# Two-layer decoder trunk: the second product of each SwiGLU by seven products of quarters

## The chip, the cores and the metric

The kernel runs on one core of one Trainium2 chip. The metric is the device time of one execution in microseconds. TensorE (PE) multiplies, VectorE (DVE) and ScalarE (ACT) do the work by elements, GpSimd (POOL) a little of the norms, and the queue of SyncE (SP) issues nearly all transfers.

## The reference, cut to what matters

The input is 512 tokens of width 1024; 16 learned meta tokens are put ahead of them, which makes 528. Two layers follow, each with a SwiGLU, a mixer and a second SwiGLU, and a last norm; the meta tokens are dropped at the end. All of it is float32.

```python
def swiglu(x, w_in, w_out):
    gate, up = jnp.split(x @ w_in, 2, axis=-1)
    return (jax.nn.silu(gate) * up) @ w_out          # D_FF = 2816

for i in range(DEPTH):                               # DEPTH = 2
    h = h + 0.5 * swiglu(rmsnorm(h, norm_ffn1[i]), ffn1_w_in[i], ffn1_w_out[i])
    hn = rmsnorm(h, norm_mix[i])
    mix = retention(hn, ...) if i == 0 else gla(hn, ...)
    h = h + mix
    h = h + 0.5 * swiglu(rmsnorm(h, norm_ffn2[i]), ffn2_w_in[i], ffn2_w_out[i])
h = rmsnorm(h, final_norm)
```

## The kernel before

The activations lie with their features on the 128 partitions and the tokens along the free axis: the residual stream `xa` is 8 row tiles of 128 x 528. The hidden layer of a SwiGLU has 22 such row tiles. The 528 tokens are taken as two halves of 264; the last SwiGLU, which needs no meta tokens, has halves of 256. The program has six stages, one after the other: the SwiGLU f10, the retention, the SwiGLUs f20 and f11, the gated linear attention, and the SwiGLU f21. The names of tiles carry these.

Every float32 product is made of three matmuls (`mm3`, L296 to L298): both factors are split into a high part and the rest, and high by high, high by rest and rest by high are added up in PSUM. The activations' parts are `uha` and `ula` (`hh` and `hl` of the hidden layer). The weights stream in by SP's queue as chunks of 128 x 1024 into four buffers (`raw`), and are split on the chip in pieces of 512 columns: ACT copies the high part (`whi`, L119) and DVE subtracts it (`wlo`, L120). Seven buffers of each part let this run up to seven pieces ahead of PE. One piece feeds four row tiles of the sum, which is 12 matmuls on one half of the tokens.

The first product of a SwiGLU (the gates `g` and the ups `u`) is taken as it stands for the first four hidden tiles. The other 18 tiles go in nine pairs by `unit`: two tiles by two halves of the tokens are a product of 2 x 2 quarters, and seven products of quarters and of their sums (Winograd's form) take the place of eight. The sums of weight quarters (`ws`, four for each unit, L105) are made by DVE ahead of the split, and those of the activations (`t_sums`) once for each SwiGLU. The three banks X, Y and Z take the products, and DVE and ACT put the quarters of the result together as they come. A pair of tiles, gate and up, is 2 x 7 pieces, or 168 matmuls.

The second product (`out_steps`) is taken as it stands: the 22 hidden tiles are cut into `GROUPS` of four or two, and for each group and each of the 8 row tiles of the result there is a step of 24 matmuls (12 for the group of two) into `po_f`, after which DVE adds half of it to `xa` (L670). The steps of a group lie between the quarters of the next group's units (`mid`, and after the unit), and those of the last group at the end, where each row tile of `xa` becomes final and `feed` makes the next stage's `uha` and `ula` (L367, L369) and the squares of the norm (L377) from it. The order on each engine is that of the program, except that what stands in `urgent()` is moved ahead of other ready work by the tile scheduler.

## Time and profile before

| | before |
|---|---|
| median of 3 runs | 2157.18 us (2157.05 to 2157.83) |
| profiled execution, its own time | 2157.2 us |
| its span | 2155.8 us |
| PE busy | 2138.7 us, 99% |
| DVE busy | 1699.6 us, 79% |
| ACT busy | 990.6 us, 46% |
| POOL busy | 20.8 us, 1% |

The profiled execution's time is that of the median run, and its span is 1.4 us shorter than it. Busy time is the time in which at least one instruction of the engine runs. The page's 40 slices show PE at nine tenths or more in all but the first and the last, and the granted clock of PE at nine tenths or more in all of them.

### The profile page before, as it was taken

What the parts mean: (1) busy time and instruction counts of PE and PEld (TensorE: products, weight loads), DVE (VectorE), ACT (ScalarE), POOL (GpSimd) and SP (SyncE); (2) the same over time, 40 slices, a digit from 0 to 9 for tenths busy, and PEclk for the clock granted to TensorE, in tenths of its full rate; (3) what the DMA queues carried; (4) which work ended last, traced back from release to release, by engine and by line L of the source; (5) the groups of instructions that cost most, each with busy time, mean ns of one, the idle gap of its engine ahead of it and who ended that gap; (6) DMA issues with size and microseconds to landing.
All of it is one profiled execution on the core that took longest, in us unless ns stands there. A gap on an engine that the chain in (4) does not pass through costs nothing.

```text
span 2155.8 us, 42829 instructions
## 1 busy us (share of the span) xinstructions
PE 2138.7 (99%) x17454; PEld 2121.4 (98%) x17454; DVE 1699.6 (79%) x3105; ACT 990.6 (46%) x1843; POOL 20.8 (1%) x25
## 2 busy tenths in 40 slices
PE   8999999999999999999999999999999999999998
PEld 8999999999999999999999999999999999999998
DVE  7887787977676788798787878787775659798886
ACT  5454445444444454454444444444633234454444
POOL 0000000000000000000000000000000000000000
PEclk9999999999999999999999999999999999999999
DMA  4333334232323222333333233333321122333332
GB/s 147 99 107 95 104 99 131 71 99 79 99 79 99 79 79 60 98 104 103 99 94 113 70 96 102 108 99 100 107 70 59 60 77 71 94 103 99 108 99 79
DMA packets 71844, 201.28 MB, mean 93 GB/s; under 512 B 8032, under 2 KB 13536, under 8 KB 71648
## 3 DMA queue, kind: packets, MB, share of 16 engines
q1 hardware_dynamic: 70640, 195.26, 29.8%
q10 hardware_dynamic: 1008, 3.29, 0.5%
q8 instruction: 137, 2.24, 0.4%
q14 instruction: 59, 0.48, 0.1%
HBM read 196.42 MB, written 2.10 MB: 92 GB/s over the span
## 4 chain that ended last, share of the span: by engine, by line
PE 97%; DVE 2%; ACT 1%; issue 0%; POOL 0%; DMA 0%; POOLq 0%; DVEq 0%; ACTq 0%
PE po_f L296 8%; PE po_f L297 8%; PE po_f L298 8%; PE po_r L298 1%; PE po_r L296 1%; PE po_r L297 1%; PE lv L1147 1%; PE po L296 1%; PE gv L296 1%; PE pk L296 1%; PE pk L297 1%; PE gv L298 1%; PE gv L297 1%; PE pk L298 1%; PE gg L296 1%; PE gg L298 1%
## 5 line engine op out<-in xcount | busy, mean ns | idle before, releaser
L119 ACT CAST whi<-raw 128x512 fp32r<-128x512 f32 (+1 forms) x653 | 397.2, 610 | 595.7 <-PE gv L297 50.0
L120 DVE TENSOR_TENSOR wlo<-raw,whi 128x512 fp32r<-128x512 f32 (+1 forms) x653 | 437.7, 673 | 94.4 <-ACT whi L119 89.5
L297 PE MATMUL po_f<-hlf,whi 128*128 128x264 f32 (+1 forms) x1344 | 380.8, 283 | 0.0
L296 PE MATMUL po_f<-hhf,whi 128*128 128x264 f32 (+1 forms) x1344 | 380.8, 283 | 0.0
L298 PE MATMUL po_f<-hhf,wlo 128*128 128x264 f32 (+1 forms) x1344 | 380.3, 283 | 0.0
L119 ACT CAST whi<-ws 128x512 fp32r<-128x512 f32 x344 | 213.1, 621 | 341.3 <-PE po_f L297 91.7
L120 DVE TENSOR_TENSOR wlo<-ws,whi 128x512 fp32r<-128x512 f32 x344 | 235.4, 685 | 23.5 <-ACT whi L119 21.4
L298 PEld LDWEIGHTS po_f<-hhf,wlo 128*128 128x128 f32 x1344 | 253.0, 188 | 0.0
L296 PEld LDWEIGHTS po_f<-hhf,whi 128*128 128x128 f32 x1344 | 253.0, 188 | 0.0
L297 PEld LDWEIGHTS po_f<-hlf,whi 128*128 128x128 f32 x1344 | 252.7, 188 | 0.0
L670 DVE SCALAR_TENSOR_TENSOR xa<-po_f,xa 128x528 f32<-128x528 f32 (+1 forms) x184 | 129.1, 701 | 109.4 <-PE po_f L298 108.7
L105 DVE TENSOR_TENSOR ws<-raw 128x512 f32<-128x512 f32 x86 | 59.3, 689 | 36.3 <-DMA raw<-in_f_in 36.2
L298 PE MATMUL po_r<-ogh,wlo 128*128 128x264 f32 x256 | 73.0, 285 | 0.0
L296 PE MATMUL po_r<-ogh,whi 128*128 128x264 f32 x256 | 72.9, 285 | 0.0
L297 PE MATMUL po_r<-ogl,whi 128*128 128x264 f32 x256 | 72.6, 284 | 0.0
L324 ACT CAST hhf<-uf 128x528 fp32r<-128x528 f32 (+1 forms) x88 | 55.3, 628 | 31.8 <-DVE uf L624 21.4
L325 DVE TENSOR_TENSOR hlf<-uf,hhf 128x528 fp32r<-128x528 f32 (+1 forms) x88 | 61.4, 699 | 3.9 <-ACT hhf L324 1.4
L105 DVE TENSOR_TENSOR ws<-ws,raw 128x512 f32<-128x512 f32 x86 | 59.0, 686 | 0.8
L105 DVE TENSOR_TENSOR ws<-raw,ws 128x512 f32<-128x512 f32 x86 | 58.8, 683 | 0.4
L105 DVE TENSOR_TENSOR ws<-raw,raw 128x512 f32<-128x512 f32 x86 | 58.7, 683 | 0.1
L296 PEld LDWEIGHTS po_r<-ogh,whi 128*128 128x128 f32 x256 | 48.3, 189 | 0.0
L297 PEld LDWEIGHTS po_r<-ogl,whi 128*128 128x128 f32 x256 | 48.3, 189 | 0.0
(647 smaller groups left out, 7065.0 us busy)
## 6 DMA issues: line engine op xcount, KB each, us to landing
raw<-in_f_in SPq DMA_DIRECT2D x176, 512.0 KB, 3.5
raw<-in_f_out SPq DMA_DIRECT2D x160, 256.0 KB, 2.7
raw<-in_ret_in SPq DMA_DIRECT2D x48, 512.0 KB, 3.5
raw<-in_gla_in SPq DMA_DIRECT2D x25, 512.0 KB, 3.5
raw<-in_ret_o SPq DMA_DIRECT2D x16, 512.0 KB, 3.5
raw<-in_f_out SPq DMA_DIRECT2D x32, 128.0 KB, 2.2
raw<-in_gla_o SPq DMA_DIRECT2D x8, 512.0 KB, 3.4
xa<-in_xT SPq DMA_DIRECT2D x8, 264.0 KB, 5.1
```

The source lines that it names most:

```text
L105: op(t, a, b)
L119: self.nc.scalar.copy(hi[:, :n], raw[:, :n])
L120: self.nc.vector.tensor_sub(lo[:, :n], raw[:, :n], hi[:, :n].bitcast(F32))
L296: nc.tensor.matmul(ps, lhsT=lh, rhs=rh, start=start, stop=False, **kw)
L297: nc.tensor.matmul(ps, lhsT=lh, rhs=rl, start=False, stop=False, **kw)
L298: nc.tensor.matmul(ps, lhsT=ll, rhs=rh, start=False, stop=stop, **kw)
L324: S.copy(hi, src)
L325: V.tensor_sub(lo, src, hi.bitcast(F32))
L670: ins = V.scalar_tensor_tensor(xv, ps[d][:, :, :wd], scale, xv, ALU.mult, ALU.add)
L1147: nc.tensor.matmul(ps[:, j, J * P:J * P + n], lhsT=Kt[:, j, J * P:(J + 1) * P], rhs=q, start=(J == 0), stop=(J == 3), skip_group_check=True)
```

## The change

The second product is taken by units of seven as well. The hidden tiles are cut into groups of 8, 8 and 6 (`GROUPS`; the last SwiGLU has 6, 6, 6 and 4, and its last group stays as it was, in `out_last`). The first four tiles of a SwiGLU are still computed as they stand (`NPL`). For a group, four units (`unit_o`) make the 8 row tiles of the result in pairs, each of 7 pieces with as many row tiles of the sum as the group has pairs of tiles: 4, 4 and 3, so a piece is 12 or 9 matmuls and 512 or 384 columns of weights. `ffn_steps` writes the order out: the four units of a group stand in a row between the gate unit and the up unit of the next group's first pair, and those of the last group at the end.

For this the hidden layer is needed as quarters: for each pair of tiles `hidden` now makes four sums of quarters on DVE (`t_sums`) and splits seven quarters in place of two tiles. The form of the seven is another one, for all units, those of the retention too: of weight quarters only sums are taken, X is one bank in which `a11`, `s2`, `s3` and `a22` are added up one after the other, and Q and Z are a pair of banks. ACT copies X after `a11` and after `s2`, and Z after `s1`; DVE reads X after `s3` (`c22`), the pair of banks after `s4` (`row1`), and X again after `a22` (`c21`). The matmuls of `a22` go into X and so follow the reading by `c22`; between `s3` and `a22` lies the piece `s4`.

In the retention, the steps of the scores (`steps`) stand ahead of the gates for every head; so far they stood inside the first gate unit for head 0. The rows of `w_out` lie in DRAM in the new order, with fewer and larger transfers: SP issues 395 where it issued 483.

```diff
-GROUPS = ((0, 4), (4, 6), (6, 10), (10, 14), (14, 18), (18, 22))
+GROUPS = ((0, 8), (8, 16), (16, 22))
+LAST_GROUPS = ((0, 6), (6, 12), (12, 18), (18, 22))
+NPL = 4
...
-    UNIT = ("a11", "s2", "s1", "s3", "a12", "s4", "a22")
-    FIRST = ("s2", "s1", "a11", "s3", "a12", "s4", "a22")
+    UNIT = ("a11", "s1", "s2", "a12", "s3", "s4", "a22")
+    FIRST = ("s1", "s2", "a11", "a12", "s3", "s4", "a22")
+    SUMS = {"s1": ("a21", "a22"), "s2": ("s1", "a11"), "s3": ("a11", "a21"), "s4": ("a12", "s2")}
...
+    def ffn_steps(last):
...
+        for gi, (f0, f1) in enumerate(groups):
+            for f in range(max(f0, NPL), f1, 2):
+                steps.append(("i", "g", f))
+                steps += outs
+                outs = []
+                steps.append(("i", "u", f))
+            plain = last and gi == len(groups) - 1
+            outs = [("l" if plain else "o", gi, d) for d in range(0, KD, 1 if plain else 2)]
+        return steps + outs
...
+                if kind == "o":
+                    W.add_unit(key, w_out[layer, b_, :, c], w_out[layer, b_ + 1, :, c], W.UNIT)
...
+    WITH = {"a11": ("n11", "X"), "s1": ("t1", "Z"), "s2": ("t2", "X"), "a12": ("n21", "Q"), "s3": ("n3", "X"),
+            "s4": ("n22", "Z"), "a22": ("t4", "X")}
...
+        for q in W.FIRST if first else W.UNIT:
+            what, into = WITH[q]
             w = W.get(key + (q,))
...
+                if q == "s1":
+                    S.copy(su[:, 2], to["Z"])
+                elif q == "a11":
+                    S.copy(su[:, int(first)], X)
+                    if first:
+                        V.tensor_sub(su[:, 0], su[:, 1], su[:, 3])
+                elif q == "s2":
+                    S.copy(su[:, 3 if first else 1], X)
+                elif q == "s3":
+                    c22(X, su[:, 2])
+                elif q == "s4":
+                    row1(su[:, :2], QZ)
+                elif q == "a22":
+                    c21(X)
...
-        for q in (W.FIRST if first else W.UNIT)[:3]:
-            quarter(q, *{"a11": ("X", "b11"), "s2": ("Y", "t2"), "s1": ("Z", "t1")}[q])
...
-        mid()
-        quarter("s3", "Y", "t3")
-        with urgent():
-            V.tensor_add(u3, ps["Y"], s1)
-        quarter("a12", "X", "b21")
-        with urgent():
-            done(0, 0, None, ps["X"])
-        quarter("s4", "Z", "b22")
-        with urgent():
-            done(0, 1, ps["Z"], u2)
-            done(1, 1, u3, s5)
-        quarter("a22", "Y", "t4")
-        with urgent():
-            done(1, 0, ps["Y"], s1)
...
+                    split(hi[:, 4], lo[:, 4], y[:, 0, a0:a1])
+                    t_sums(up_, f"{me}h{f}", halves, y[:, 0], y[:, 1], h[:, 0, :4], h[:, 1, :4])
+                    split(hi[:, 5:], lo[:, 5:], pair(y[:, 1], halves))
...
+            def unit_u(f, g):
...
+                def row1(ab, qz):
+                    o = pair(y[0][:, 0], halves)
+                    V.tensor_add(o, ab, qz)
+                    V.tensor_mul(o, o, pair(g[0], halves))
...
+                def c22(c, s):
+                    y.append(gated(f))
+                    o = y[0][:, 1, b0:b1]
+                    V.tensor_add(o, c, s)
+                    V.scalar_tensor_tensor(o, o, -1.0, g[1][:, b0:b1], ALU.mult, ALU.mult)
...
+                def c21(c):
+                    V.scalar_tensor_tensor(y[0][:, 1, a0:a1], c, -1.0, g[1][:, a0:a1], ALU.mult, ALU.mult)
...
+            def unit_o(gi, d):
...
+                def row1(ab, qz):
+                    o = pair(x[d], halves)
+                    V.scalar_tensor_tensor(o, ab, -0.5, o, ALU.mult, ALU.add)
+                    ins = V.scalar_tensor_tensor(o, qz, -0.5, o, ALU.mult, ALU.add)
+                    if feed and gi == len(groups) - 1:
+                        feed(d, ins)
...
+                def c22(c, s):
+                    o = x[d + 1][:, b0:b1]
+                    V.scalar_tensor_tensor(o, s, 0.5, o, ALU.mult, ALU.add)
+                    V.scalar_tensor_tensor(o, c, 0.5, o, ALU.mult, ALU.add)
...
+                def c21(c):
+                    o = x[d + 1][:, a0:a1]
+                    ins = V.scalar_tensor_tensor(o, c, 0.5, o, ALU.mult, ALU.add)
+                    if feed and gi == len(groups) - 1:
+                        feed(d + 1, ins)
```

Two places show how the instructions move. The first is DVE's queue in the middle of the SwiGLU f20, at the end of an up unit: `Xf20u`, `Yf20u`, `Zf20u` and `QZf20u` are PSUM, `suf20u` is the copies of quarters in SBUF, `uf` and `yf` are gated hidden tiles, and `gf` the gates. Before:

```order
L120 TENSOR_TENSOR wlo_12993<-ws_208_12990,whi_12992 128x512
L624 TENSOR_TENSOR uf_12761<-uf_12761,gf_12556 128x264
L623 TENSOR_TENSOR uf_12762<-Yf20u_12764,suf20u_12766 128x264
L120 TENSOR_TENSOR wlo_13010<-raw_12746,whi_13009 128x512
L624 TENSOR_TENSOR uf_12762<-uf_12762,gf_12557 128x264
L325 TENSOR_TENSOR hlf_12967<-uf_12761,hhf_12966 128x528
L325 TENSOR_TENSOR hlf_12967<-uf_12762,hhf_12966 128x528
L670 SCALAR_TENSOR_TENSOR xa<-po_f_12934,xa 128x528
L120 TENSOR_TENSOR wlo_13029<-ws_208_13026,whi_13028 128x512
```

After:

```order
L640 TENSOR_TENSOR yf_12833<-suf20u_12739,QZf20u_12738 128x528
L122 TENSOR_TENSOR wlo_12924<-ws_168_12921,whi_12923 128x512
L641 TENSOR_TENSOR yf_12833<-yf_12833,gf_12600 128x528
L650 SCALAR_TENSOR_TENSOR yf_12833<-Xf20u_12737,gf_12601 128x264
L463 TENSOR_TENSOR ttf20h_12876<-yf_12833 128x264
L340 TENSOR_TENSOR hf_12873<-yf_12833,hf_12873 128x264
L464 SCALAR_TENSOR_TENSOR ttf20h_12876<-yf_12833,ttf20h_12876 128x264
L465 TENSOR_TENSOR ttf20h_12876<-yf_12833 128x264
L466 SCALAR_TENSOR_TENSOR ttf20h_12876<-yf_12833,ttf20h_12876 128x264
L340 TENSOR_TENSOR hf_12873<-yf_12833,hf_12873 128x528
L122 TENSOR_TENSOR wlo_12943<-raw_12661,whi_12942 128x512
L122 TENSOR_TENSOR wlo_12962<-raw_12777,whi_12961 128x512
```

The update of `xa` between the splits is gone, and the two splits of whole hidden tiles have become four sums of quarters (`ttf20h`, L463 to L466) and three splits (L340).

The second place is DVE's queue at the end of f20, where the last group's product makes `xa` final. Before, step by step:

```order
L120 TENSOR_TENSOR wlo_14898<-raw_14689,whi_14897 128x512
L369 SCALAR_TENSOR_TENSOR ula<-xa,gains,uha 128x528
L377 TENSOR_TENSOR sqa_n_10266<-sqa_n_10266,sq_n_4_14881 128x528
L670 SCALAR_TENSOR_TENSOR xa<-po_f_14813,xa 128x528
L120 TENSOR_TENSOR wlo_14975<-raw_14723,whi_14974 128x512
L369 SCALAR_TENSOR_TENSOR ula<-xa,gains,uha 128x528
L377 TENSOR_TENSOR sqa_n_10266<-sqa_n_10266,sq_n_5_14917 128x528
L670 SCALAR_TENSOR_TENSOR xa<-po_f_14850,xa 128x528
L120 TENSOR_TENSOR wlo_14979<-raw_14723,whi_14978 128x512
L670 SCALAR_TENSOR_TENSOR xa<-po_f_14884,xa 128x528
```

After, in the third and fourth of the last four units:

```order
L122 TENSOR_TENSOR wlo_14868<-raw_14717,whi_14867 128x384
L672 SCALAR_TENSOR_TENSOR xa<-Xf20o_14805,xa 128x264
L122 TENSOR_TENSOR wlo_14883<-ws_198_14880,whi_14882 128x384
L665 SCALAR_TENSOR_TENSOR xa<-QZf20o_14806,xa 128x528
L107 TENSOR_TENSOR ws_198_14897<-ws_198_14880,raw_14717 128x384
L676 SCALAR_TENSOR_TENSOR xa<-Xf20o_14805,xa 128x264
L384 SCALAR_TENSOR_TENSOR ula<-xa,gains,uha 128x528
L392 TENSOR_TENSOR sqa_n_10304<-sqa_n_10304,sq_n_4_15028 128x528
L384 SCALAR_TENSOR_TENSOR ula<-xa,gains,uha 128x528
L392 TENSOR_TENSOR sqa_n_10304<-sqa_n_10304,sq_n_5_15048 128x528
```

One update of a whole row tile (L670) has become, for a pair of row tiles, two of 528 elements and three of 264 (L664 to L676), and two row tiles become final together, with the split of the next stage's input (L384) and the squares (L392) of both behind them.

## Rows read from the trace of the kernel before

**Rows 1.** The page's head and part 1: busy us, share of span, instructions.

```profile
span 2155.8 us, 42829 instructions
PE 2138.7 (99%) x17454; PEld 2121.4 (98%) x17454; DVE 1699.6 (79%) x3105; ACT 990.6 (46%) x1843; POOL 20.8 (1%) x25
```

**Rows 2.** The page's part 4: the chain that ended last, its shares by engine.

```profile
PE 97%; DVE 2%; ACT 1%; issue 0%; POOL 0%; DMA 0%; POOLq 0%; DVEq 0%; ACTq 0%
```

**Rows 3.** Waits of PE: operation, releaser, us in total, times, longest.

```profile
PE pf10g L296 <- ACT whi L119: 6.2, 1, 6.2
...
PE bc_n L423 <- DVE dg_n L416: 0.5, 1, 0.5
```

**Rows 4.** Busy us by windows: length, PE, PEld, DVE, ACT, POOL; clock, DMA.

```profile
820.00:840.00 20.00, 20.00 (x166) 20.00 (x165) 20.00 (x30) 9.40 (x13) 0.00 (x0) 1.00 0.14 49
860.00:1164.00 304.00, 304.00 (x2500) 304.00 (x2499) 245.28 (x440) 143.05 (x272) 0.00 (x0) 1.00 0.35 103
1935.00:2107.00 172.00, 172.00 (x1458) 172.00 (x1457) 141.34 (x256) 81.49 (x157) 0.00 (x0) 1.00 0.34 103
```

**Rows 5.** Timeline of DVE, first SwiGLU: start us, duration us, line, operation.

```profile
206.99 0.69 DVE L120 TENSOR_TENSOR wlo<-raw,whi 128x512 fp32r<-128x512 f32 x1
207.59 0.68 DVE L105 TENSOR_TENSOR ws<-ws,raw 128x512 f32<-128x512 f32 x1
```

**Rows 6.** Timeline of DVE, end of the retention and start of f20.

```profile
810.71 0.71 DVE L670 SCALAR_TENSOR_TENSOR xa<-po_r,xa 128x528 f32<-128x528 f32 x1 [1.62 <-PE po_r L298]
811.34 0.76 DVE L369 SCALAR_TENSOR_TENSOR ula<-xa,gains,uha 128x528 fp32r<-128x528 f32 x1
812.01 0.70 DVE L377 TENSOR_TENSOR sqa_n<-sqa_n,sq_n 128x528 f32<-128x528 f32 x1
812.63 0.77 DVE L369 SCALAR_TENSOR_TENSOR ula<-xa,gains,uha 128x528 fp32r<-128x528 f32 x1
...
815.38 0.23 DVE L412 TENSOR_SCALAR ms_n<-st_n 128x4 f32<-128x4 f32 x2 [0.77 <-PE st_n L403]
816.73 0.78 DVE L416 TENSOR_TENSOR dg_n<-ident,rc 128x512 f32<-128x512 f32 x2 [1.12 <-POOL rc L414]
...
819.62 0.71 DVE L558 TENSOR_TENSOR gf<-pf20g,rb 128x528 f32<-128x528 f32 x1 [0.33 <-ACT rb L424]
...
826.67 1.25 DVE L325 TENSOR_TENSOR tlf<-ttf,thf 128x1056 fp32r<-128x1056 f32 x1
827.84 0.42 DVE L558 TENSOR_TENSOR gf<-pf20g,rb 128x264 f32<-128x264 f32 x1
828.18 1.24 DVE L325 TENSOR_TENSOR tlf<-ttf,thf 128x1056 fp32r<-128x1056 f32 x1
```

**Rows 7.** Timeline of DVE, start of f10.

```profile
5.71 0.77 DVE L369 SCALAR_TENSOR_TENSOR ula<-xa,gains,uha 128x528 fp32r<-128x528 f32 x1 [4.70 <-ACT uha L367]
...
22.56 0.23 DVE L412 TENSOR_SCALAR ms_n<-st_n 128x4 f32<-128x4 f32 x2 [1.28 <-PE st_n L403]
...
24.30 0.78 DVE L416 TENSOR_TENSOR dg_n<-ident,rc 128x512 f32<-128x512 f32 x2 [0.91 <-POOL rc L414]
...
28.11 0.71 DVE L558 TENSOR_TENSOR gf<-pf10g,rb 128x528 f32<-128x528 f32 x1 [2.44 <-ACT rb L424]
```

**Rows 8.** Timeline of PE, first unit of f10: its third piece begins.

```profile
62.55 0.28 PE L296 MATMUL Xf10g<-uha,whi 128*128 128x264 f32 x1
```

**Rows 9.** Timeline of PE, first unit of f20: its third piece begins.

```profile
862.60 0.28 PE L296 MATMUL Xf20g<-uha,whi 128*128 128x264 f32 x1
```

**Rows 10.** Timeline of PE and DVE, f10: a quarter that DVE reads.

```profile
199.81 0.28 PE L298 MATMUL Zf10g<-uha,wlo 128*128 128x264 f32 x1
...
200.14 0.43 DVE L616 TENSOR_TENSOR gf<-Zf10g,suf10g 128x264 f32<-128x264 f32 x1 [0.21 <-PE Zf10g L298]
```

**Rows 11.** Waits: operation, releaser, us in total, times, longest.

```profile
DVE ws L105 <- DMA raw<-in_f_in: 36.2, 53, 2.0
```

**Rows 12.** Issues of DMAs: what, queue, count, KB each, median us to landing.

```profile
raw<-in_f_in SPq DMA_DIRECT2D x176, 512.0 KB, 3.5
```

More of the change, by code (lines that the diff above doesn't have):

```diff
@@ new lines, in sums, with renorm @@
+            def sums(j):
+                norm(j)
+                for i in range(2):
+                    k = 2 * j + i
+                    t_sums(up_, f"{me}{k}", halves, normed[j][:, 0, i, :], normed[j][:, 1, i, :], th[:, k], tl[:, k])
+            def renorm():
+                for h, r0, r1 in ((0, a0, a1), (1, a0, a1), (1, b0, b1)):
+                    for j in range(2):
+                        k = 4 * h + 2 * j
+                        split(uha[:, k:k + 2, r0:r1], ula[:, k:k + 2, r0:r1], normed[j][:, h, :, r0:r1])
@@ new lines, in evac, with plain @@
+                V.scalar_tensor_tensor(y[:, f % 2, a0:], up[:, a0:], -1.0, sg[:, a0:], ALU.mult, ALU.mult)
+                if f % 2:
+                    hidden(f - 1, y)
+                for j in (((0,), (1,), (), ()) if late else ((1,), (), (), ()))[f]:
+                    sums(j)
+            def plain(s, f, ps, outs):
+                w = W.get((which, layer, "p", s, f))
+                if (2 * f + (s == "u")) % 3 < 2:
+                    t = acc_tile(f"p{me}{s}{f}")
+                    ps[s] = [t[:, hf, :wd] for hf in range(2)]
+                    outs[s] = [(t[:, :, :wd], lambda t: pair(t, halves))]
+                else:
+                    ps[s] = [bank(f"p{me}{s}{f}{hf}")[:, :wd] for hf in range(2)]
+                    outs[s] = [(ps[s][hf], lambda t, hf=hf: t[:, halves[hf][0]:halves[hf][1]]) for hf in range(2)]
+                for hf, (r0, r1) in enumerate(halves):
+                    proj(ps[s][hf], w, 0, KD, uh, ul, (r0, r1))
+                    if hf == 1:
+                        W.free(w)
+                    hook()
@@ new lines, in unit_g @@
+            def unit_g(f, first):
+                g = gates(f)
+                def row1(ab, qz):
+                    o = pair(g[0], halves)
+                    V.tensor_add(o, ab, qz)
+                    S.activation(o, o, AF.Silu, scale=-1.0)
+                def c22(c, s):
+                    o = g[1][:, b0:b1]
+                    V.tensor_add(o, c, s)
+                    S.activation(o, o, AF.Silu)
+                def c21(c):
+                    S.activation(g[1][:, a0:a1], c, AF.Silu)
+                unit((which, layer, "i", "g", f), f"{me}g{f}", first, halves, 4, rhs_in, up_, row1, c22, c21)
+                return g
@@ new lines, in ffn @@
+            first, ps, outs, g = True, {}, {}, None
+            for kind, a_, b_ in ffn_steps(feed is None):
+                if kind == "p":
+                    s, f = a_, b_
+                    if s == "g":
+                        before, ps, outs = outs, {}, {}
+                    plain(s, f, ps, outs)
+                    if (s, f) == ("g", 0) and not late:
+                        drain_pending()
+                        sums(0)
+                    if (s, f) == (("g", 1) if late else ("u", 0)):
+                        drain_pending()
+                        evac(0, before if late else outs)
+                    if s == "u" and f:
+                        evac(f, outs)
+                    if (s, f) == ("u", NPL - 1):
+                        renorm()
+                elif kind == "i":
+                    if a_ == "g":
+                        g = unit_g(b_, first)
+                        first = False
+                    else:
+                        unit_u(b_, g)
+                elif kind == "o":
+                    unit_o(a_, b_)
+                else:
+                    hs = H[a_]
+                    out_last(lambda d: (which, layer, "l", len(groups) - 1, d),
+                             [h[:, 0, i, :] for i in range(2) for h in hs], [h[:, 1, i, :] for i in range(2) for h in hs],
+                             halves, -0.5)
+                    break
```

337 lines of the change are left out of this document (138 added, 199 removed).

## The prediction

> **What bounds the kernel now.** I read the page's busy times first: TensorE is busy for 2138.7 of 2155.8 us, VectorE for 79% and ScalarE for 46% [rows 1]. The chain that ended last is TensorE's for 97% [rows 2], and its longest single wait is 6.2 us at the start, for the first weights; the next kind that I use is 0.5 us [rows 3]. In 304 us of the third stage TensorE and its weight loads never stop, at a granted clock of 1.00 [rows 4]. So the time is a count of matmuls times their pitch: 304.00 / 2500 = 0.1216 us for 264 columns, and in the last SwiGLU 172.00 / 1458 = 0.118 us for 256 [rows 4]. What takes matmuls away gains, until another engine is late.
>
> VectorE is that engine, so I price its work by the distance between starts, not by the durations, which overlap: 0.60 us for 512 elements a partition [rows 5], 0.62 for 528, 0.67 to 0.69 for 528 with a gain (0.68 below), 1.17 for 1056, 0.34 for 264 [rows 6]. For 384 elements, which no row shows, the bounds are 0.34 and 0.60; I take 0.47, by the straight line between them. In the same 304 us VectorE is busy for 245.28, and ScalarE for 143.05 [rows 4].
>
> **The change part by part.** The profiled execution takes 2157.2 us, 1.4 of them outside the span, which I leave as they are; it is the median run, so the sum is made against 2157.2.
>
> *1. Matmuls taken away.* A second product had 8 row tiles x 22 hidden tiles x 2 halves x 3 = 1056 matmuls. Now it has 4 pairs of row tiles x 7 quarters x (4 + 4 + 3) x 3 = 924. The first product keeps its 384 + 9 x 168. So 132 go in each of three SwiGLUs: 132 x 0.1216 = 16.05 us, 48.2 together. In f21 there are 4 x 7 x 9 x 3 + 8 x 4 x 2 x 3 = 948, so 108 go, at 0.118: 12.7. Sum: -61.0 us. That the units are not there after all, so that the change doesn't do what it says, is excluded by the order: TensorE's queue holds these counts.
>
> *2. VectorE beside a pair of the first product.* Before, a pair of units with its four output steps was 264 matmuls, 32.1 us, beside some 24.2 us of VectorE. Now the output units stand apart, and the pair has its 168 matmuls, 20.43 us. VectorE has 14 splits and 8 weight sums (22 x 0.60 = 13.2), the gates (0.62 + 0.34 = 0.96), the ups (2 x 0.62 + 3 x 0.34 = 2.26) and the hidden layer's sums and splits (5 x 0.34 + 0.62 + 1.17 = 3.49): 19.9 us, or 97%. An output unit of four pairs has 84 matmuls, 10.21 us, beside 11 x 0.60 + 2 x 0.62 + 3 x 0.34 = 8.9; one of three pairs 63 matmuls, 7.66, beside 11 x 0.47 + 2.26 = 7.4. By these sums VectorE just keeps up. The new risk is X: `c22` must have read it before the matmuls of `a22`, one piece of 12 matmuls (1.46 us) after `s3` ends. VectorE starts 0.2 us after the last matmul of what it reads [rows 10], one instruction in front may cost up to 0.60 and reading takes 0.43; the slack is 1.46 - 0.2 - 0.43 - 0.1 = 0.7 us. A delay is also made up in the output units. Bounds for each of the 36 pairs: nothing, and one wait for weights, 36.2 / 53 = 0.68 us by the row of such waits [rows 11], paid in full. A gain is excluded, since TensorE was already without gaps. I take 0.2 us a pair, near the lower end, because VectorE is busy for all of 20.00 us at the start of f20 while TensorE issues 166 matmuls without a loss [rows 4]: 36 x 0.2 = +7 (0 to 25).
>
> *3. The ends of f10, f20 and f11.* The last group's four units (252 matmuls, 30.6 us) lie beside everything that makes `xa` final. From the last quarter of the last up unit VectorE has the rest of the ups and the hidden layer (5.3), 29 splits and sums of 384 (13.6), 2 splits of 512 (1.2), the updates of `xa` (8 x 0.62 + 12 x 0.34 = 9.0), six splits of the next stage's input (4.1) and five sums of squares (3.1): 36.3 us. VectorE is some 6 us behind at the end, three times: +18. The bounds come from the price of 384 elements: at 0.34 it is 2 us, at 0.60 it is 9.5, so 6 to 28. Before, the same final work was spread over steps of 24 matmuls, 2.9 us each, with one update, split, sum of squares and weight split (2.6). f21 has no next stage and keeps its last group plain: nothing.
>
> *4. The starts.* VectorE now has the hidden layer's quarters of four plain tiles to make before the first unit. In f10 it starts at 5.71 [rows 7], has 61.3 us of work up to its first `c22` by the order (28 of 512, 25 of 528, 16 of 528 with a gain, 31 of 264, 6 of 1056, some small), and idles for 1.28 + 0.91 + 2.44 = 4.6 for the norm [rows 7]; it gets to `c22` at 71.3. TensorE's first unit begins two pieces before 62.55 [rows 8], at 59.6, and its fifth piece ends 7.3 later: 67.1 with the 0.2 of [rows 10]. The lag of 4.2 less the slack of 0.7 is about 4. In f20 VectorE starts the last update at 810.71, has 54.2 us and idles of 0.77 + 1.12 + 0.33 = 2.2 [rows 6]: 866.8 at `c22`, against TensorE's 862.60 - 2.9 + 7.3 + 0.2 = 867.2 [rows 9]: nothing. f11 has 56.9 us with the same idles, 58.8 against f20's stretch of 49.0 + 7.3 + 0.2 = 56.5: 2.3 less 0.7, about 2. Sum: +6 (0 to 12).
>
> *5. At nothing.* ScalarE's load goes from some 155 to 195 us a SwiGLU of 343, which TensorE covers; without cover it is 40 us each. The retention has the same matmuls, and VectorE 11 us less in its units. SP issues 395 transfers where it issued 483, each hidden by the raw buffers; without that cover a landing is 3.5 us [rows 12]. `steps` of head 0 moves ahead of the gates, with the same work.
>
> Sum: 2157.2 - 61.0 + 7 + 18 + 6 = **2127 us**.
>
> **The rivals.** *All is covered.* The seven buffers let VectorE fall behind by some pieces, and TensorE stays dense: only some 8 us of parts 2 to 4 are paid, so 2157.2 - 61 + 8 = 2104 (2096 to 2109). For it: the dense 20 us at full VectorE [rows 4]. Against: part 3's lag is on the way to the next stage's input, which no weight buffer shortens.
>
> *The gain is eaten.* VectorE bounds the four SwiGLUs throughout: each of 36 pairs takes 0.5 us and each of 48 output units 0.3 us more than counted, by small waits for ScalarE's copies and splits. In place of part 2's 7 stand 18 + 14, and the time is 2120 + 32 = 2152 (2147 to 2161). For it: 97% leaves VectorE 0.5 us a pair. Against: where VectorE was full before, TensorE lost nothing [rows 4].
>
> *Slower.* VectorE waits, ahead of a weight sum, for chunks that land late: before, it did so 53 times, 0.68 us on average and 2.0 at most [rows 11], and had 8 us free beside each pair to make it up. Now a slot of `raw` comes free some 3.6 us of VectorE's work ahead of the first sum that reads its next chunk, a landing takes 3.5 [rows 12], and what is queued behind the waiting sum on VectorE are the splits and then `c22`, for which the matmuls of `a22` wait. If three of a pair's four chunks are late, a pair loses 3 x 0.68 - 0.5 = 1.5 us; 36 of them are 55, and the time is 2120 + 55 = 2175 (2162 to 2200). From (2161.5 - 2120) / 36 = 1.15 us a pair on, the kernel is slower than before. For it: the narrow margin. Against: a VectorE that runs late finds its weights already there, so that waits don't add up.
>
> *Every VectorE instruction at its full duration.* Starts lie 0.60 apart where a duration is 0.69 [rows 5], so an instruction starts before the one ahead has ended. If that were not so where instructions depend on each other more closely, as in the new hidden layer, each would cost 0.08 more; 620 instructions a SwiGLU are 51 us, VectorE would have 386 us against TensorE's 343, and the time would be 2157.2 - 61 + 4 x 43 = 2268. The rows speak against it.
>
> The Trainium skill, "VectorE: DVE Perf Modes", section "The DRAIN you can't avoid", states that the next VectorE instruction does not start until the pipe is empty, and adds that one which is not held starts earlier; the first half would make the time that of this rival, and the trace's starts, 0.60 apart, are those of the second.
>
> **How the numbers follow.** The forecast has 0.62, with 2110 to 2146 as its own range from the bounds of parts 2 to 4, which are not likely to be met all at once; all covered 0.14; the gain eaten 0.09; slower by late weights 0.13; full durations 0.02. The range of 2102 to 2158 leaves out a third of the covered case below (0.04) and the two slow cases above (0.15), with an edge of the eaten gain. About 0.2%, or 4.3 us, is what a measurement of this kernel can tell from no change, so 2152.9 is the bound of faster and 2161.5 that of slower. The forecast, the covered case and a third of the eaten gain are faster, 0.79; the rest of the eaten gain and a trace of the slow case are the same, 0.07; slower has 0.14.
>
> **What would show it.** Right: TensorE's matmul count lower by 504, gaps of some 6 us at the three turns of stages with VectorE as the releaser, about 4 us in X of f10's first unit, hardly anything in the pairs, VectorE near 95% in the SwiGLUs. Wrong: turns without a gap (part 3), waits of `a22` for `c22` in most pairs (part 2), waits of VectorE for transfers with TensorE behind them (the slower rival), or distances between VectorE's starts above those of the rows.

## The result and the profile after

The change takes 2142.77 us (median; 2141.96 to 2145.85) where the kernel before takes 2157.14 in the same runs: a ratio of 0.9935, with an interval of 0.9921 to 0.9949. The time lies in the range of the prediction and on the side that it gave, but the gain is 14.4 us, where 30 were forecast.

The page of the changed kernel, its first line, part 1 and the shares of part 4, which answer to [rows 1] and [rows 2]:

```profile
span 2140.2 us, 42535 instructions
PE 2103.9 (98%) x16950; PEld 2069.3 (97%) x16950; DVE 1868.0 (87%) x3451; ACT 1146.0 (54%) x2220; POOL 21.8 (1%) x25
PE 79%; DVE 15%; ACT 2%; DMA 2%; issue 2%; POOL 0%; SPq 0%; DVEq 0%; POOLq 0%; ACTq 0%
```

TensorE issues 504 matmuls less (17454 to 16950). VectorE goes from 79% to 87% and owns 15% of the chain that ended last, where it owned 2%. The waits of TensorE (operation, releaser, us in total, times, longest) answer to [rows 3]:

```profile
PE pf10g L311 <- ACT whi L121: 5.7, 1, 5.7
PE pf10g L313 <- DVE wlo L122: 4.7, 2, 3.6
PE Xf10o L311 <- ACT whi L121: 2.7, 3, 1.2
PE Xf20o L311 <- ACT whi L121: 2.7, 3, 1.2
PE Xf11o L311 <- ACT whi L121: 2.7, 3, 1.2
...
PE pg_gz L1150 <- ACT whi L1143: 1.1, 1, 1.1
PE pf11g L313 <- DVE wlo L122: 1.1, 1, 1.1
...
PE QZrg L311 <- DVE pl L340: 0.4, 2, 0.2
```

The second product's units (names with `o`) wait for high parts of weights, f10's plain tiles for the rest of theirs. Windows of the last group's units of f10 and of the middle of f20 (length, then busy us of PE, PEld, DVE, ACT, POOL) answer to [rows 4]:

```profile
336.10:372.90 36.80, 33.96 (x254) 31.64 (x254) 36.27 (x73) 25.14 (x54) 0.00 (x0) 1.00 0.25 77
865.00:1125.00 260.00, 259.93 (x2124) 258.75 (x2123) 247.56 (x442) 155.43 (x307) 0.00 (x0) 1.00 0.32 102
```

In f10's last units VectorE is busy for 36.27 of 36.80 us and TensorE stops; in the middle of f20 VectorE is at 95% and TensorE hardly stops.

Where the time went can be laid out whole. For each matmul I took the distance to the next one's start and subtracted the pitch of its width (0.1216 us for 264 columns, 0.118 for 256, and in the mixers a fixed figure for each width, the same for both kernels). What is left, summed by stretch, is the time that TensorE lost there:

| stretch | lost before, us | lost after, us | more | forecast |
|---|---|---|---|---|
| first weights and plain tiles of f10 | 4.8 | 13.1 | +8.4 | +4 |
| plain tiles of f20, f11, f21 | 1.9 | 4.7 | +2.8 | +2 |
| 36 pairs of the first product | 0.6 | 5.7 | +5.0 | +7 |
| last units of f10, f20, f11 (6.1, 6.1, 6.3) | 0.4 for all steps | 18.6 | +18.6 | +18 |
| the other 36 units of the second product | in the line above | 6.7 | +6.4 | 0 |
| retention | 9.2 | 12.0 | +2.8 | 0 |
| linear attention | 6.2 | 7.6 | +1.4 | 0 |
| the last, plain product of f21 | 0.7 | 1.3 | +0.7 | 0 |
| sum | 23.8 | 69.7 | +45.9 | +31 |

The column "more" is rounded row by row, so that its rows add up to 46.1.

The matmuls taken away are worth 3 x 132 x 0.1216 + 108 x 0.118 = 60.9 us, as forecast, and the first matmul starts 0.6 us earlier. 60.9 + 0.6 - 45.9 = 15.6 is the difference of the two spans, 2155.8 and 2140.2. It is more than the 14.4 of the medians because the profiled execution of the changed kernel is its fastest, 2141.96 us.

### The profile page after: what moved, and what is told of

Same layout as the page of the kernel before. It is cut to its first block, busy times and chain, and to the rows that moved or that the text cites. A ratio compares the mean times of both kernels' runs of the same rounds, so it can differ in the third digit from the quotient of the medians.

```text
span 2140.2 us, 42535 instructions
## 1 busy us (share of the span) xinstructions
PE 2103.9 (98%) x16950; PEld 2069.3 (97%) x16950; DVE 1868.0 (87%) x3451; ACT 1146.0 (54%) x2220; POOL 21.8 (1%) x25
## 4 chain that ended last, share of the span: by engine, by line
PE 79%; DVE 15%; ACT 2%; DMA 2%; issue 2%; POOL 0%; SPq 0%; DVEq 0%; POOLq 0%; ACTq 0%
DVE wlo L122 4%; DVE ws L107 2%; PE po_r L313 1%; PE po_r L311 1%; PE po_r L312 1%; PE lv L1227 1%; DVE hf L340 1%; PE Xf21o L311 1%; PE Xf20o L311 1%; DMA raw<-in_f_in 1%; PE Xf20g L311 1%; PE Xf20g L312 1%; PE Xf20g L313 1%; PE Xf20u L311 1%; PE Xf11g L311 1%
## 5 line engine op out<-in xcount | busy, mean ns | idle before, releaser
L121 ACT CAST whi<-ws 128x512 fp32r<-128x512 f32 (+1 forms) x536 | 322.3, 603 | 340.9 <-DVE ws L107 86.8
L122 DVE TENSOR_TENSOR wlo<-ws,whi 128x512 fp32r<-128x512 f32 (+1 forms) x536 | 349.5, 659 | 27.6 <-ACT whi L121 25.5
L107 DVE TENSOR_TENSOR ws<-raw 128x512 f32<-128x512 f32 (+1 forms) x134 | 88.6, 661 | 20.1 <-DMA raw<-in_f_in 13.6
L107 DVE TENSOR_TENSOR ws<-ws,raw 128x512 f32<-128x512 f32 (+1 forms) x134 | 88.6, 661 | 1.6
L107 DVE TENSOR_TENSOR ws<-raw,raw 128x512 f32<-128x512 f32 (+1 forms) x134 | 88.3, 659 | 0.4
L107 DVE TENSOR_TENSOR ws<-raw,ws 128x512 f32<-128x512 f32 (+1 forms) x134 | 88.2, 658 | 0.4
L311 PE MATMUL Xf10o<-hf,whi 128*128 128x264 f32 x176 | 51.1, 291 | 2.9 <-ACT whi L121 2.7
L311 PE MATMUL Xf11o<-hf,whi 128*128 128x264 f32 x176 | 51.1, 291 | 2.9 <-ACT whi L121 2.7
L311 PE MATMUL Xf20o<-hf,whi 128*128 128x264 f32 x176 | 51.1, 291 | 2.8 <-ACT whi L121 2.7
L313 PE MATMUL Xf20o<-hf,wlo 128*128 128x264 f32 x176 | 50.3, 286 | 0.0
L312 PE MATMUL Xf10o<-hf,whi 128*128 128x264 f32 x176 | 50.1, 285 | 0.0
L312 PE MATMUL Xf11o<-hf,whi 128*128 128x264 f32 x176 | 50.0, 285 | 0.0
L312 PE MATMUL Xf20o<-hf,whi 128*128 128x264 f32 x176 | 50.0, 285 | 0.0
L340 DVE TENSOR_TENSOR hf<-yf,hf 128x264 fp32r<-128x264 f32 (+2 forms) x86 | 49.3, 573 | 0.6 <-ACT hf L339 0.5
```

The costliest lines, as they stand in the source:

```text
L107: V.tensor_add(t, a, b)
L121: self.nc.scalar.copy(hi[:, :n], raw[:, :n])
L122: self.nc.vector.tensor_sub(lo[:, :n], raw[:, :n], hi[:, :n].bitcast(F32))
L311: nc.tensor.matmul(ps, lhsT=lh, rhs=rh, start=start, stop=False, **kw)
L312: nc.tensor.matmul(ps, lhsT=lh, rhs=rl, start=False, stop=False, **kw)
L313: nc.tensor.matmul(ps, lhsT=ll, rhs=rh, start=False, stop=stop, **kw)
```

## The experiments

All times are medians; ratios are to the kernel before, which took 2157.2 to 2157.8 us beside them. "The changed kernel" is the one of the result.

### The last group made larger

```diff
-GROUPS = ((0, 8), (8, 16), (16, 22))
+GROUPS = ((0, 6), (6, 14), (14, 22))
```

> One edit to the changed kernel: the groups of hidden tiles of f10, f20 and f11 are 6, 8 and 8 in place of 8, 8 and 6, with the same count of matmuls. The last group's units then have 84 matmuls (10.2 us) each beside 11 x 0.60 + 2.26 + 2.6 = 11.5 us of VectorE, where they had 63 (7.7) beside 10.0. Theory of the amount (the prediction's part 3): the loss at each end, 7.0 to 7.6 us in the changed kernel, is VectorE's work above TensorE's, 40.1 against 40.9 us now, so that it falls to about 1 us; the first group's units, with 63 matmuls now, cost about 1 us as those of f21 do. Sum 3 x (-6 + 1) = -15, with 1 more at the turn to the fifth stage: 2127 (2123 to 2132). Rival: four units in a row with the feed lose a fixed time by the chain from weight sum to copy to split, whatever their size: 2142.8 within 2.

2124.08 us, a ratio of 0.9846 (0.9830 to 0.9863): 18.7 us less than the changed kernel, by one line and with the same matmuls. The last units lose 1.9 us in each SwiGLU where they lost 6.1 to 6.3; the turns behind them lose less too (f11's plain tiles 0.6 where it was 3.4, the linear attention 6.2 where it was 7.6). The window of f10's last units, and the wait of TensorE there:

```profile
322.10:364.90 42.80, 41.80 (x338) 41.17 (x337) 42.30 (x76) 28.82 (x56) 0.00 (x0) 1.00 0.29 94
```

```profile
PE Xf10o L311 <- ACT whi L121: 0.9, 2, 0.6
```

VectorE is still full, 42.30 of 42.80 us, but TensorE has 41.8 us of work beside it in place of 34.0. A fixed loss for a row of units is ruled out: what counts is either VectorE's work against TensorE's or the longer piece (12 matmuls in place of 9), and the next run separates the two.

### The additions of squares left out

```diff
-                V.tensor_add(sq[:, t0:], sq[:, t0:], t[:, t0:])
+                if add:
+                    V.tensor_add(sq[:, t0:], sq[:, t0:], t[:, t0:])
...
-                squared(d - 2)
+                squared(d - 2, False)
```

> The changed kernel with the additions of squares left out wherever feed calls them (the norms then rest on the squares of the first row tile alone; ScalarE still makes the squares). VectorE loses 7 x 0.62 = 4.3 us at each turn of stages, 5 of them, 3.1 us, inside the last group's units of f10, f20 and f11. It is the run with GpSimd without GpSimd. Theory of the amount: each of the three ends loses 3 us less (7.2 becomes about 4), the start of the next stage a little too: 2142.8 - 9 = 2134 (2131 to 2136). Rival: the ends are bound by the chain from weight sum to copy to split, and groups of 8 helped because a piece of 12 matmuls gives that chain more time: 2142.8 within 2.

This kernel leaves out part of every such norm; it serves the question alone. 2129.63 us (0.9870; 0.9854 to 0.9887), 13.1 less than the changed kernel and a little more of a gain than the range of the expectation. Each row of last units loses 4.0 us, 2.1 to 2.3 less, and the rest comes behind them: f11's plain tiles 0.6 in place of 3.4, the linear attention 5.4 in place of 7.6, f10's plain tiles 10.9 in place of 13.1 (1.2 of these 2.2 us are a shorter stretch at the lower clock, see the part on the starts). The window of f10's last units:

```profile
333.80:368.60 34.80, 33.26 (x256) 31.49 (x255) 34.62 (x70) 25.73 (x56) 0.00 (x0) 1.00 0.30 96
```

It is VectorE's again (34.62 of 34.80), and 2 us shorter. The pieces are as in the changed kernel, so the loss goes by VectorE's amount and not by what a piece gives the chain to copy and split; of the 3.1 us taken off VectorE, 2.1 to 2.3 come back here.

### The same additions on GpSimd

```diff
-                V.tensor_add(sq[:, t0:], sq[:, t0:], t[:, t0:])
+                G.tensor_tensor(sq[:, t0:], sq[:, t0:], t[:, t0:], ALU.add)
```

> One edit to the changed kernel: the running sums of squares for the norms (7 additions of 528 elements at each of the six turns) are made by GpSimd in place of VectorE. Theory of the amount: 5 of them, 3.1 us, lie on VectorE in the last group's units of f10, f20 and f11, so each end's loss falls by about 3: 2142.8 - 9 = 2134 (2131 to 2137). Rival: GpSimd's additions are slow and late, the norm waits for them, and the plain stretch of the next stage loses what the end gained: 2143 to 2155. Third: the ends are bound by the chain from weight sum to copy to split, not by VectorE's amount: 2142.8 within 1.5.

2168.14 us (1.0051; 1.0036 to 1.0066): 25 us slower than the changed kernel, and 38.5 slower than with the additions left out. None of the three expectations reached that far. Three things can be told apart. TensorE waits 8.9 us for the sums. Then, the granted clock falls to 0.50, the lower of its two levels (1.2 GHz), in seven stretches, three at such waits, three in the last units and one in f10's plain tiles, each beside a stop of TensorE; 109 matmuls start 0.22 us apart there in place of 0.12, which is 10.7 us over the pitch, where the changed kernel has one such stretch with 22 matmuls and 2.2 us. One of the seven, in f20's last units (length, busy us of PE, PEld, DVE, ACT, POOL, then the granted clock):

```profile
1179.20:1185.90 6.70, 6.11 (x28) 6.11 (x29) 4.68 (x11) 3.81 (x8) 0.00 (x0) 0.50 0.61 189
```

And the last units of f10, f20 and f11 lose 10.8 to 12.0 us each where they lost 6.1, some of it at that clock. What VectorE has to do with that stands in the timeline of f10's end (start, duration, engine):

```profile
355.58 0.55 DVE L107 TENSOR_TENSOR ws<-ws,raw 128x384 f32<-128x384 f32 x1
355.60 1.73 POOL L392 TENSOR_TENSOR sqa_n<-sqa_n,sq_n 128x528 f32<-128x528 f32 x1 [327.78 <-issue]
356.05 1.69 DVE L122 TENSOR_TENSOR wlo<-ws,whi 128x384 fp32r<-128x384 f32 x1
...
361.08 1.32 POOL L392 TENSOR_TENSOR sqa_n<-sqa_n,sq_n 128x528 f32<-128x528 f32 x1 [3.76 <-ACT sq_n L391]
361.13 1.68 DVE L107 TENSOR_TENSOR ws<-raw,ws 128x384 f32<-128x384 f32 x1
...
362.80 1.89 POOL L392 TENSOR_TENSOR sqa_n<-sqa_n,sq_n 128x528 f32<-128x528 f32 x1 [0.40 <-ACT sq_n L391]
363.42 1.56 DVE L671 SCALAR_TENSOR_TENSOR xa<-suf10o,xa 128x264 f32<-128x264 f32 x1
```

While GpSimd adds, one instruction of VectorE takes 1.56 to 1.69 us in place of 0.55 for 384 elements (and 0.43 for 264). In the whole run 25 instructions are hit, 27.5 us in all, where 42 additions of 0.62 us, 26 us, were taken off VectorE: it has no less to do than before, and TensorE waits for the sums on top. All that are hit read two inputs from SBUF. The Trainium skill says so ("GPSIMD Engine Reference", section "1. Specifications": the SBUF interfaces are shared with VectorE, with contention for instructions that have two inputs in SBUF), without a price; the trace agrees and gives one. GpSimd's own addition takes 1.3 to 1.9 us.

### The activation sums one tile later

```diff
-                for j in (((0,), (1,), (), ()) if late else ((1,), (), (), ()))[f]:
+                for j in (((0,), (), (1,), ()) if late else ((), (1,), (), ()))[f]:
```

> One edit to the changed kernel: the second half of the sums of activation quarters (sums(1)) is called one plain hidden tile later, after the third in f10 and after the second in the other SwiGLUs. In the changed kernel the plain stretch of f10 loses 13.1 us to distances above the pitch, 5.2 of them in two waits of pf10g for wlo at 48.3 and 53.7 us, and that of f11 3.4, one of 1.3 at 1197. Theory of the order: VectorE has the time, but the splits of plain weight pieces stand behind four products with rb and eight sums in its queue; then the two waits go, f10's plain stretch falls to about 8 us, f11's to about 2, and the time to 2142.8 - 6 = 2137 (2135 to 2139). Theory of the amount (the prediction's part 4): VectorE has too much work up to the first unit; then the loss comes back as waits at the first unit or its c22, and the time stays at 2142.8 within 1.5.

2142.23 us (0.9930; 0.9915 to 0.9944), no difference. The two waits of f10's plain tiles for `wlo` went, and the loss came back in its first units: 6.7 in the plain tiles and 9.9 in the pairs, 16.6 together where it was 15.2. Both kernels have a stretch at the lower clock behind stops of TensorE; here it lies in the first units, from 69.6 to 76.3, with a granted clock of 0.50. The largest of TensorE's waits in those units is now:

```profile
PE QZf10g L312 <- DVE ula L340: 2.2, 2, 1.1
```

The theory of the order fell; VectorE has too much to do before the first unit, and the order only says where TensorE pays. f11's plain tiles lost 1.6 in place of 3.4.

### Six plain tiles in f10

```diff
-        steps = [("p", s, f) for f in range(NPL) for s in "gu"]
+        steps = [("p", s, f) for f in range(npl) for s in "gu"]      # npl: 6 in f10, else 4
...
-                if f % 2:
+                if f % 2 and (f < npl - 1 or npl == NPL):
                     hidden(f - 1, y)
-                for j in (((0,), (1,), (), ()) if late else ((1,), (), (), ()))[f]:
+                for j in (((0,), (), (1,), (), (), ()) if late else ((1,), (), (), ()))[f]:
...
+                        if npl > NPL:
+                            hidden(npl - 2, ys[npl - 2])
```

> The kernel with groups of 6, 8 and 8, and in f10 alone six hidden tiles as they stand in place of four, with the second half of the activation sums one tile later. TensorE gets 24 matmuls more, 2.9 us. A plain pair has 192 matmuls, 23.3 us, beside some 12 us of VectorE, so that VectorE can make up 11 us ahead of the first unit. Theory of the amount: the 12.1 us lost in f10's plain stretch and first units fall to the 5 that were lost before the change (first weights) plus 1: 2124 - 6 + 2.9 = 2121 (2119 to 2123). Rival: the loss comes from the start of VectorE itself (waits for the norm and the order of the splits), and stays: 2127.

The edit also moves work: the second half of the sums comes one tile later, and the hidden layer of the last plain pair is made behind the splits of `renorm`. 2121.32 us (0.9831; 0.9817 to 0.9846). By the trace f10's plain tiles and pairs lose 8.2 us where they lost 12.1 in the run with groups of 6, 8 and 8; of that, 2.9 go into the added matmuls and 0.2 into later units, which leaves 0.7. About 1.2 of the 3.9 us are the clock: in the run with groups of 6, 8 and 8 it is granted at 0.50 from 52.3 to 55.6, with 12 matmuls 0.22 us apart, and here at 1.00 throughout f10. More time ahead of the first unit goes with a smaller loss, as the amount says, but not with the 5 or 6 expected, and the new order may have its share, which no run separates. The difference of the medians, 2.8, is not clear of the intervals.

### Single banks in the retention

```diff
-        QZ = acc_tile(f"QZ{name}")[:, :, :wd]
+        if single:
+            QZ = [bank(f"{b}{name}")[:, :wd] for b in "QZ"]
+        else:
+            QZ = acc_tile(f"QZ{name}")[:, :, :wd]
```

> The kernel with groups of 6, 8 and 8, and in the retention's units Q and Z in two single banks in place of a pair of banks, which the scores use too; row1 is then two instructions of 264 in place of one of 528 there. The retention lost 12.2 us above the pitch against 9.2 before the change; four waits of about 0.4 us stand where QZ's first matmul waits for the split pl of the scores, and sc waits 0.73 where it waited 0.48. Theory of the banks: QZ's waits go, 4 x 0.4 = 1.6, and the retention is at 10.6: 2124 - 1.6 = 2122.5. Rival: the later place of steps is the cause; then the retention stays at 12.2 and the time at 2124.

2120.85 us (0.9827; 0.9812 to 0.9842). The retention loses 10.3 us where it lost 12.2; the medians lie 3.2 apart, but their intervals overlap, so that the trace has to tell. TensorE's waits there in the run with groups of 6, 8 and 8:

```profile
PE sc L311 <- DVE pl L340: 2.8, 5, 0.7
...
PE QZrg L311 <- DVE pl L340: 0.7, 3, 0.3
```

and in this one, with no other for the units:

```profile
PE sc L311 <- DVE pl L340: 2.7, 5, 0.7
```

The pair of banks that Q and Z share with the scores cost about 2 of the retention's 2.8 us. What is left of it stands where `sc` waits (1.3 us in the kernel before, 2.7 here) and `bc_ro` (0.7 before, 1.6 here); why was not tried.

### The new form without units in the second product

```diff
-                if kind == "o":
-                    W.add_unit(key, w_out[layer, b_, :, c], w_out[layer, b_ + 1, :, c], W.UNIT)
-                else:
-                    W.add(key, w_out[layer, b_, :, c])
+                W.add(key, w_out[layer, b_, :, c])
...
-                    unit_o(a_, b_)
+                    todo[b_]()      # todo: out_steps on the whole tiles of the group
```

> The changed kernel with the second product taken as it stands again: eight steps in a row for each group (48 matmuls each for a group of 8, 36 for 6), the hidden layer split as whole tiles, no sums of its quarters; groups, order and the new form of the units stay. It tells what the new form alone costs, and what the seven quarters of the second product give. By TensorE's counts and the losses measured by section: the matmuls of before, the retention's 2.8 us, f10's start at 2 to 4 in place of 8.4, ends without loss: 2157.2 + 2.8 + 3 = 2163 (2159 to 2166); the units of the second product are then worth about 20 us net. Rival: the new form's longer X (c22 before a22) and the outputs in a row cost by themselves: 2167 to 2180, and then the units of the second product give more than 24 us.

2174.07 us (1.0075; 1.0060 to 1.0090), 16 slower than the kernel before. So the new form and the order cost 16 us by themselves, and the units of the second product give 31 us net of their own losses: the rival was right. By stretches it loses 3.0 more than the kernel before in f10's plain tiles, 4.5 in the pairs, 1.7 in the steps of each of f10, f20 and f11, 1.4 in the second product of f21 and 2.5 in the retention, 16.5 in all. The waits of TensorE:

```profile
PE po_f L309 <- DVE hf L337: 2.4, 3, 0.8
PE sc L308 <- DVE pl L337: 2.0, 4, 0.6
PE pf10g L310 <- DVE wlo L122: 1.6, 1, 1.6
```

The last group's steps wait for the hidden tiles of the last pair, which they need at once; in the kernel before, a step of the group ahead of them lay between the last unit and them.

### All gains together, and groups of 8, 6, 4 and 4 in f21

The edits of groups, plain tiles and banks in one kernel, and the same with

```diff
-LAST_GROUPS = ((0, 6), (6, 12), (12, 18), (18, 22))
+LAST_GROUPS = ((0, 8), (8, 14), (14, 18), (18, 22))
```

> The edits that gave time together: groups of 6, 8 and 8, six plain hidden tiles in f10 with the second half of the activation sums one tile later, and single banks for Q and Z in the retention. If they lie in different stages and add up: the kernel with groups of 6, 8 and 8 at 2124, less 1.9 us in the retention, less 0.7 in f10: 2121 (2118 to 2123). If the retention's gain is given back at the next turn of stages: 2124.

> The run with all edits, with f21's groups 8, 6, 4 and 4 in place of 6, 6, 6 and 4; the count of matmuls is the same, 948. It tests whether VectorE's amount by group size holds for f21: by distances between starts a unit of four pairs has 9.9 us of matmuls (84 x 0.118) beside 8.9 of VectorE, one of three 7.4 beside 7.4, one of two 5.0 beside 11 x 0.34 + 2.26 = 6.0. Theory of the amount: four units of two pairs lose 1.0 each, four of four pairs nothing, four of three 1 in all as now: f21's units lose about 5 in place of 3, +2 us on the run with all edits. Rival: a loss per group, whatever its size: no change.

2120.89 us (0.9829; 0.9816 to 0.9842) and 2123.41 us (0.9837; 0.9824 to 0.9851). Together they come out at the 2121 expected of them, but no faster than each with the new groups alone, within what the runs can tell; the retention's loss stayed at 10.3. f21 with unequal groups lost 2.9 us more by the trace, near the 2 that the amount gave, though not where I put it: its pairs went from 2.2 to 5.7 and its units from 3.0 to 2.4. That VectorE carries its arrears into the next pair would fit that, but it is not shown, and the medians, 2.5 apart, are not clear of each other.

### The units in the middle: splits asked for earlier, and X read by ScalarE

Units that VectorE can keep up with lost 0.2 us each. Two causes were tried on the run with all edits:

```diff
-AHEAD = 4
+AHEAD = 6
```

> The run with all edits, with the weight splits asked for six pieces ahead in place of four (AHEAD); the seven buffers stay. It asks why the units of the second product in the middle of a SwiGLU lose some 0.2 us each, of which the prediction saw nothing. If their first pieces are only just in time because the splits are asked for late, the 6 us of these units and the 5 of the pairs are roughly halved: 2121 - 5 = 2116 (2114 to 2119). If VectorE's amount sets it, an earlier request moves no work: 2121 within 2, or later where the splits push what frees PSUM behind.

```diff
-                    V.scalar_tensor_tensor(o, c, 0.5, o, ALU.mult, ALU.add)
+                    S.copy(spare, c)
+                    V.scalar_tensor_tensor(o, spare, 0.5, o, ALU.mult, ALU.add)
```

> The run with all edits, with one more in the units of the second product: after s3 ScalarE copies X into a free quarter in SBUF, and VectorE adds from there, so that the matmuls of a22 wait for ScalarE in place of VectorE. It asks whether the units in the middle of a SwiGLU lose their 5.6 us (0.16 each) because c22 reads X late: the weight loads of Xf10o to Xf21o wait for c22's line 13 times and 2.8 us in the changed kernel, and a restart adds about 0.1 us each time. If so, and ScalarE is free when s3 ends: the middle units lose about 2 in place of 5.6, 2121 - 3.5 = 2117.5 (2116 to 2119). If ScalarE is as late as VectorE, behind its splits: 2121 within 1.5. If the copies push the high parts of the weights back: 2122 to 2126.

Earlier splits: 2119.92 us (0.9826; 0.9809 to 0.9842), and 6.4 us lost in the middle units where it was 7.0: no difference. X copied by ScalarE: 2115.94 us (0.9806; 0.9790 to 0.9823), 4.95 less than the run with all edits, and 2.6 us lost there, 4.4 less. The lines that showed the way are the weight loads' waits in the changed kernel (operation, releaser, us in total, times, longest):

```profile
PEld Xf21o L311 <- DVE xa L672: 1.0, 4, 0.4
...
PEld Xf11o L311 <- DVE xa L672: 0.7, 3, 0.3
...
PEld Xf20o L311 <- DVE xa L672: 0.6, 3, 0.2
PEld Xf10o L311 <- DVE xa L672: 0.5, 2, 0.3
```

`xa` L672 is `c22`'s reading of X, and the load that waits is that of `a22`. In the run with ScalarE's copy no unit of the second product waits for VectorE any more; the longest left in f10's is

```profile
PEld Xf10o L311 <- ACT whi L121: 0.8, 1, 0.8
```

This is the fastest kernel of the study, 41 us below the kernel before.

## Why the prediction came out as it did

**The matmuls taken away** were right: 504 of them, 60.9 us.

**Part 3, the ends,** was right in mechanism and size: +18 forecast, 18.6 measured. 384 elements take 0.465 to 0.48 us from start to start, where 0.47 was taken, and the runs with other groups and without squares move the loss the way VectorE's count does. TensorE's waits there name ScalarE's copies (`whi`), and these can come late because VectorE does: ahead of the copy that TensorE waits for at 1161.44 (last section), ScalarE stood idle for 2 us at the next stage's input,

```profile
1158.00 0.74 ACT L382 ACTIVATE uha<-xa,gains 128x528 fp32r<-128x528 f32 x1 [2.01 <-DVE xa L665]
```

which needs VectorE's update of `xa`. Whether another order on ScalarE would take some of the loss away was not tried.

**Part 2, the pairs,** was right: +7 forecast, 5.0 measured, so the rival by late weights never came up; VectorE's waits for landings of weights of the first product fell from the 53 of [rows 11] to

```profile
DVE ws L107 <- DMA raw<-in_f_in: 13.6, 20, 1.1
```

What failed in part 2 is the sentence that an output unit makes up a delay, and so costs nothing. The wait that I priced, that of `a22`'s matmuls for `c22`, falls in the output units: 36 of them lost 6.4 us, and the run in which ScalarE takes X away shows it for 4.4 of the 7.0 us that they lose in the run with all edits. In f21 a piece has 9 matmuls and leaves 1.06 - 0.2 - 0.43 - 0.1 = 0.3 us of slack by the prediction's own terms, where 0.7 was counted for 12: its 12 units lost 2.9 us, the other 24, with pieces of 12, lost 3.9.

**Part 4, the starts,** was right for f20 (nothing). f11 cost 2.8 for 2, but that was luck: in the run with groups of 6, 8 and 8, which leaves f11's start as it is, its plain tiles lose 0.6, so that the 2.8 go with f20's end and not with the work ahead of `c22` alone. f10 cost 8.4 for 4. Two terms were too small there: VectorE's idle time, and the clock, which the prediction had at its full level for every matmul. VectorE's queue at f10's start, to be held against [rows 7] (in square brackets, idle us ahead and the releaser):

```profile
4.67 0.77 DVE L384 SCALAR_TENSOR_TENSOR ula<-xa,gains,uha 128x528 fp32r<-128x528 f32 x1 [3.66 <-ACT uha L382]
...
28.13 0.71 DVE L591 TENSOR_TENSOR sgf<-pf10g,rb 128x528 f32<-128x528 f32 x1 [3.01 <-ACT rb L439]
...
50.45 0.42 DVE L464 SCALAR_TENSOR_TENSOR ttf<-unf,ttf 128x264 f32<-128x264 f32 x1
50.79 0.42 DVE L465 TENSOR_TENSOR ttf<-unf 128x264 f32<-128x264 f32 x1
51.13 0.42 DVE L466 SCALAR_TENSOR_TENSOR ttf<-unf,ttf 128x264 f32<-128x264 f32 x1
51.48 0.68 DVE L122 TENSOR_TENSOR wlo<-raw,whi 128x512 fp32r<-128x512 f32 x1
...
61.96 0.71 DVE L591 TENSOR_TENSOR sgf<-pf10g,rb 128x528 f32<-128x528 f32 x1 [1.94 <-PE pf10g L313]
...
75.20 0.43 DVE L626 TENSOR_TENSOR gf<-Xf10g,suf10g 128x264 f32<-128x264 f32 x1
```

It starts at 4.67, reaches `c22` at 75.20 in place of 71.3, with 62.1 us of work (61.3 forecast) and 8.4 us idle, where I summed 4.6 from the three longest waits. 3.0 stand in front of the first product with rb, several small ones were left out, and 1.94 at 61.96 come from TensorE, which was late itself. TensorE pays 3.8 of its loss earlier than I put it, at a plain tile whose split stands behind the sums in VectorE's queue (51.48 above), and 1.4 more at 53.65 for the next split. Then it runs slowly: the granted clock is 0.50 (1.2 GHz) from 53.7 to 60.4 and 1.00 (2.4 GHz) behind that, and matmuls start 0.22 us apart in place of 0.12. 22 such distances are 2.2 us over the pitch. In the kernel before, and in the runs with six plain tiles, TensorE doesn't stop here, and the clock stays at 1.00; in the runs with groups of 6, 8 and 8, without squares and with single banks it stops for 3.6 us as here, and the clock falls. Matmuls of the stop and of the slow stretch, then the granted clock by windows:

```profile
48.31 0.28 PE L312 MATMUL pf10u<-ula,whi 128*128 128x264 f32 x1
52.21 0.39 PE L313 MATMUL pf10g<-uha,wlo 128*128 128x264 f32 x1 [3.62 <-DVE wlo L122]
...
55.54 0.42 PE L311 MATMUL pf10g<-uha,whi 128*128 128x264 f32 x1
55.76 0.42 PE L312 MATMUL pf10g<-ula,whi 128*128 128x264 f32 x1
```

```profile
53.70:60.40 6.70, 5.61 (x26) 5.29 (x26) 6.32 (x11) 2.34 (x5) 0.00 (x0) 0.50 0.51 159
60.50:67.20 6.70, 6.70 (x57) 6.70 (x56) 5.24 (x9) 3.57 (x7) 0.00 (x0) 1.00 0.00 0
```

An estimate from these numbers closes the sum. Without the 1.94, which TensorE's own lateness made, VectorE is at `c22` at 73.26; by the prediction's working, with the first matmul 0.6 earlier, TensorE is there at 66.5. The lag of 6.8 less the slack of 0.7 is 6.1, and with the 2.2 at the lower clock 8.3 of the 8.4 measured.

**Part 5, at nothing,** was wrong by 4.9 us: the retention 2.8, two thirds of it by the pair of banks (its matmuls are the same, but not what they wait for), the turn into the linear attention 1.4, which is the end of f11 once more (it goes with larger groups), and 0.7 in f21's last product, whose cause is open.

Together: 4.4 + 0.8 at the starts, 0.6 at the ends, 6.4 in the middle units, 4.9 in part 5, less 2 in the pairs: 15 of the 30 us that were forecast. The rival "all is covered" is refuted by the ends, and the one of full durations by starts 0.34 apart with durations of 0.42 (50.45 to 51.13 above); "the gain is eaten" is nearer than I gave it, since half was.

## What to carry to other kernels

When matmuls are traded for work by elements, count the other engine's work against TensorE's in each stretch, at the smallest unit and at the ends, not over the stage: there the run was decided, and swapping a short last group for a long one gave more (18.7 us) than the whole change (14.4). A wait for PSUM to be read is only covered by the matmuls that lie between, so it has to be sized for the shortest piece that the plan contains. A stop of TensorE can cost more than its length, when the granted clock falls behind it. Moving work to an idle engine pays only if it doesn't slow the instructions of the busy one.
